# Conditioning rows formed earlier, norm sums on another engine, and two blocks' down weights in one buffer

## The chip, the cores and the metric

The kernel runs on one core of one Trainium2 chip. The metric is the device time of one execution in microseconds (us). Three timed runs of the kernel before gave 1670.92, 1672.65 and 1677.95 us, so the median is 1672.65 us. One more execution was recorded by the hardware profiler; it is the source of every row below.

A core has five instruction streams that run side by side and wait for each other through semaphores: PE (the matrix engine; its weight loads are shown as PEld), DVE (vector), ACT (scalar activation), POOL (a slower general engine) and SP (here only a queue that issues transfers). ACT and POOL issue transfers too. Each stream executes its instructions strictly in the order in which they stand: an instruction that waits holds up everything behind it on its engine, and on SP a transfer whose buffer isn't free yet holds up every later transfer of that queue.

## The reference, cut to what matters

One decoder layer on 1024 tokens of width 1024, all in float32. A conditioning vector gives six rows of 1024 numbers by one matrix product (`mod`), and these rows shift, scale and gate the two halves of the layer.

```python
cond = jax.nn.silu(c)
mod = (cond @ w_ada[layer] + b_ada[layer])[:, None, :]
sh1, sc1, gt1, sh2, sc2, gt2 = jnp.split(mod, N_MOD, axis=-1)
h = _rmsnorm(x, g_mix[layer]) * (1.0 + sc1) + sh1
x = x + gt1 * _hybrid_mixer(h, positions, rel_bias, w_in[layer], g_q_lora[layer],
                            w_uq[layer], g_kv_lora[layer], w_ukv[layer],
                            w_up_a[layer], w_up_b[layer], w_o[layer])
h = _rmsnorm(x, g_ffn[layer]) * (1.0 + sc2) + sh2
x = x + gt2 * _swiglu(h, w_gate[layer], w_up[layer], w_down[layer])
return _rmsnorm(x, g_final)
```

The mixer projects `h` by `w_in` into keys, queries, values, two gates and the latent rows `c_q` and `c_kv`; `c_q` goes through an RMS norm of its own, whose sums of squares the change touches. Two attentions follow, then `w_o`, then SwiGLU: `(silu(h @ w_gate) * (h @ w_up)) @ w_down`.

## The kernel before, in words

Activations lie transposed, features on the 128 partitions and tokens along the free axis in two halves of 512. A float32 product is made of three matmuls on a high and a low part of each operand (`split`, L82: ACT writes the high part, L83; DVE the rest, L84). The large products are done by a Strassen scheme (class `Strassen`, L168) of seven products over a 2 by 2 grid instead of eight. For that, POOL forms sums of weight quarters (`Wsum`, L190), ACT and DVE split them into operands (`Wop`, six buffers), and PE multiplies them with seven prepared operands of the right side (L220), 12 matmuls of 512 columns for a product, and 6 in the down projection. Results gather in banks of PSUM; ACT copies some out (`keep`, L163), DVE adds and combines the others (L233, L386).

The program is written in one order, and a scheduler in the compiler sets the final order of each engine's stream from it. A change at one place can therefore move instructions elsewhere too.

The stages, by the profile's time:

1. Start (0 to some 110 us): conditioning vector, first norm, the first products. The shift and scale rows of the first half are formed here (`mod_in`, L450).
2. Input projection (to 440 us): nine groups of two blocks (class `In`, loop from L702). The first eight blocks take five products each, since two were done ahead, the other ten take seven. Each block loads 1 MB of raw weights (`Wraw<-win`, L182) into one of two buffers. Beside the products run small "chores" (class `Chores`, L688): bias tables, rotary angles, the norm of `c_kv` and, by `mod_load` and `mod_run` (L666 to L678), the conditioning rows. `Chores(items, ahead, start, stop)` spreads its items over the slots from start to stop, seven slots to a group. One conditioning item handles 128 of the 1024 numbers of a row: it loads 512 KB of `w_ada` in two halves (L159, buffers `cm` and `cl` in turn), multiplies each with the conditioning vector held in two `sg` tiles (`cond_load`, L661) and sums on DVE (L675), and adds the bias (L676). In the kernel before, rows 2, 3 and 4 are formed here, 24 items from slot 30 on.
   In `cq_out` (L340) the squares of `c_q` are summed up over six blocks and two halves in `acc`; the adds stand on POOL (L348).
3. Attention (to 830 us), merge and `w_o` (to some 990 us).
4. Gate and up products (to some 1422 us): 11 pairs of blocks (class `Pair`, L1105). A pair's result is split into seven operands and stored to HBM by 14 transfers that ACT issues (`tod`, L1163). Two blocks were begun ahead and their partial results parked (`sp`), from where `post` (L1172) reloads them. In this loop (from L1206) the kernel before forms row 5, the gate of the second half: it reloads the conditioning vector (`x<-cnd`, L1205) into two of the 22 `x` buffers, and after each of the last eight pairs loads a `w_ada` block into two more and runs `mod_run`.
5. Down projection (1422 to some 1627 us): five chunks of the inner width, four blocks each (class `Down`, L1231). Two blocks run side by side, so there are ten rounds of 14 products (84 matmuls). Each block loads 512 KB of raw weights (`Wraw<-wdown`) into one of the two raw buffers of 1 MB, of which it uses half. DVE adds the result, scaled by row 5, onto the residual `x1` (L1241), which is reloaded from HBM (`x<-x1d`) as the stage begins.
6. Last blocks, final norm and output (to the end at 1674 us). Their weights (`wdl`, L1279) take a raw buffer too.

## Time and profile before

| what | value |
|---|---|
| median of three timed runs | 1672.65 us (1670.92 to 1677.95) |
| the profiled execution: its own time | 1676.03 us |
| its span, first to last instruction | 1674.2 us |
| PE busy | 1537.7 us, 92% of the span |
| PE weight loads | 1278.2 us, 76% |
| DVE busy | 1240.5 us, 74% |
| ACT busy | 829.8 us, 50% |
| POOL busy | 561.5 us, 34% |
| granted TensorE clock, mean | 0.965 of full speed |
| bytes moved | 321.92 MB, mean 192 GB/s |

A busy PE sums over the whole span; what counts in each stage is where PE stands still and what ended that. The line numbers are those of the kernel before. A row of a timeline merges equal instructions that follow each other closely. The clock has two levels, 2.4 GHz (shown as 1.00) and 1.2 GHz.

### The profile page before, as it was taken

The page shows a single profiled execution, that of the slowest core. Times are in us where ns is not written, and L with a number is a line of the kernel's source. Part 1 is how long each engine was busy: PE and PEld are TensorE (multiplying, and loading weights), DVE is VectorE, ACT ScalarE, POOL GpSimd, SP SyncE. Part 2 cuts the span into 40 slices and gives each one's busy share as a digit, 9 for nine tenths or more (in the row PEclk, how much of TensorE's full clock was granted, in tenths as well). Part 3 has the DMA queues.
Part 4 walks back from the last instruction along what each step waited for, and adds up shares of the span by engine and source line. Part 5 has one row for each costly group of instructions (what it writes and reads, how often), then busy time and mean ns, then how long its engine had stood idle before and what let it go on. Part 6 is the DMA issues. An engine that isn't in the chain of part 4 may idle for free.

```text
span 1674.2 us, 22241 instructions
## 1 busy us (share of the span) xinstructions
PE 1537.7 (92%) x7306; PEld 1278.2 (76%) x7306; DVE 1240.5 (74%) x2433; ACT 829.8 (50%) x1631; POOL 561.5 (34%) x515
## 2 busy tenths in 40 slices
PE   4989997999779989999999998989999999899996
PEld 2758786877668778999878876768888887688775
DVE  7986669576368657989866678767777786688887
ACT  5743334444467767878733563434444443222324
POOL 0143524424244546433141134322233222222323
PEclk9989999999879999999999998999999999999997
DMA  9438457558997878766195422554454449866412
GB/s 329 178 119 310 160 188 233 172 165 251 295 223 201 202 186 206 189 164 152 46 345 171 151 100 87 178 203 167 175 187 161 152 160 353 324 247 256 154 51 101
DMA packets 175652, 321.92 MB, mean 192 GB/s; under 512 B 37020, under 2 KB 72524, under 8 KB 170288
## 3 DMA queue, kind: packets, MB, share of 16 engines
q1 hardware_dynamic: 107376, 241.75, 42.2%
q0 software_dynamic: 48000, 42.04, 11.7%
q10 hardware_dynamic: 20160, 36.71, 5.8%
q8 instruction: 58, 0.95, 0.2%
q14 instruction: 58, 0.48, 0.1%
HBM read 222.73 MB, written 102.34 MB: 194 GB/s over the span
## 4 chain that ended last, share of the span: by engine, by line
PE 43%; DVE 8%; DMA 8%; ACT 3%; issue 2%; POOL 1%; ACTq 0%; SPq 0%; DVEq 0%; POOLq 0%
PE bk L220 25%; PE acc L892 3%; PE S L783 3%; PE bk L87 3%; PE bk L88 3%; PE bk L89 3%; PE pv L824 2%; DMA Wraw<-wdown 2%; DVE Wop L84 2%; PE tr L805 2%; DMA vbd<-ev 2%; DMA tod<-x 1%; DVE x L1241 1%; DVE cell L84 1%; DMA actd<-x 1%
## 5 line engine op out<-in xcount | busy, mean ns | idle before, releaser
L220 PE MATMUL bk<-cell,Wop 128*128 128x512 f32 x4056 | 951.5, 396 | 51.5 <-DVE x L233 11.0
L220 PEld LDWEIGHTS bk<-cell,Wop 128*128 128x128 f32 x4056 | 771.8, 191 | 225.1 <-ACT x L163 15.1
L190 POOL TENSOR_TENSOR Wsum<-Wraw 128x512 f32<-128x512 f32 (+1 forms) x120 | 156.4, 1304 | 599.0 <-DVE Wop L84 272.2
L83 ACT CAST Wop<-Wsum 128x512 fp32r<-128x512 f32 (+1 forms) x241 | 130.6, 550 | 198.9 <-PE bk L220 117.3
L83 ACT CAST Wop<-Wraw 128x512 fp32r<-128x512 f32 (+2 forms) x182 | 105.6, 593 | 212.4 <-PE bk L220 75.3
L84 DVE TENSOR_TENSOR Wop<-Wsum,Wop 128x512 fp32r<-128x512 f32 (+1 forms) x241 | 155.3, 653 | 61.1 <-ACT Wop L83 60.6
L84 DVE TENSOR_TENSOR Wop<-Wraw,Wop 128x512 fp32r<-128x512 f32 (+2 forms) x182 | 152.3, 843 | 39.5 <-ACT Wop L83 35.8
L783 PE MATMUL S<-cell,cell 128*128 128x128 f32 (+8 forms) x480 | 119.3, 364 | 9.7 <-DMA cell<-ksd 5.5
L1241 DVE SCALAR_TENSOR_TENSOR x<-bk,modc,x 128x512 f32<-128x512 f32 x140 | 103.5, 744 | 20.1 <-PE bk L220 18.8
L84 DVE TENSOR_TENSOR pl<-tr,ph 128x512 fp32r<-128x512 f32 (+1 forms) x160 | 98.4, 630 | 23.9 <-ACT ph L83 22.9
L790 ACT ACTIVATE P<-P,mx 128x512 f32<-128x512 f32 (+7 forms) x128 | 99.3, 778 | 29.5 <-DVE mx L785 17.6
L892 PE MATMUL acc<-cell,w 128*128 128x512 f32 x408 | 112.0, 402 | 0.1
L190 POOL TENSOR_TENSOR Wsum<-Wraw,Wsum 128x512 f32<-128x512 f32 (+1 forms) x60 | 78.5, 1313 | 68.9 <-DVE Wop L84 66.1
L805 PE MATMUL tr<-ident,P 128*128 128x128 f32 x576 | 94.1, 281 | 5.9 <-ACT P L793 5.3
L163 ACT COPY x<-bk 128x512 f32<-128x512 f32 x92 | 52.7, 588 | 91.0 <-PE bk L220 48.1
L87 PE MATMUL bk<-cell,Wop 128*128 128x512 f32 (+1 forms) x240 | 92.3, 385 | 3.7 <-ACT Wop L83 1.9
L824 PE MATMUL pv<-ph,v 128*128 128x256 f32 (+1 forms) x320 | 88.9, 294 | 6.9 <-ACT ph L83 5.6
L783 PEld LDWEIGHTS S<-cell,cell 96*128 96x128 f32 (+1 forms) x480 | 80.8, 196 | 18.6 <-DMA cell<-ksd 5.9
L88 PE MATMUL bk<-cell,Wop 128*128 128x512 f32 (+1 forms) x240 | 91.7, 383 | 0.0
L83 ACT CAST ph<-tr 128x512 fp32r<-128x512 f32 (+1 forms) x160 | 83.3, 545 | 16.3 <-PE tr L805 13.5
L89 PE MATMUL bk<-cell,Wop 128*128 128x512 f32 (+1 forms) x240 | 90.3, 379 | 0.0
L824 PE MATMUL pv<-pl,v 128*128 128x256 f32 x320 | 83.0, 294 | 4.5 <-DVE pl L84 4.1
(255 smaller groups left out, 2221.1 us busy)
## 6 DMA issues: line engine op xcount, KB each, us to landing
tod<-x ACTq DMA_DIRECT2D x140, 256.0 KB, 2.9
cell<-tod SPq DMA_DIRECT2D x70, 512.0 KB, 6.8
Wraw<-win SPq DMA_DIRECT2D x18, 1024.0 KB, 6.6
Wraw<-wgate SPq DMA_DIRECT2D x11, 1024.0 KB, 5.5
Wraw<-wup SPq DMA_DIRECT2D x11, 1024.0 KB, 6.0
Wraw<-wdown SPq DMA_DIRECT2D x20, 512.0 KB, 6.6
ada<-wada SPq DMA_DIRECT2D x16, 512.0 KB, 6.1
cell<-ksd POOLq DMA_DIRECT2D x16, 512.0 KB, 21.4
```

The lines of the kernel that those rows point to most:

```text
L83: ACT.copy(hi, src)
L84: eng.tensor_sub(lo, src, f32(hi))
L87: PE.matmul(ps, w[0], a[0], start=first, stop=False)
L88: PE.matmul(ps, w[0], a[1], start=False, stop=False)
L89: PE.matmul(ps, w[1], a[0], start=False, stop=last)
L190: POOL.tensor_tensor(t, a, b, op=op)
L220: PE.matmul(ps, w[:, wi, k], t[k][:, ti], start=start and k == 0 and n == 0, stop=k == self.nk - 1 and n == 2, skip_group_check=True)
L783: anchor[0] = PE.matmul(s, q[:, i * P:i * P + P], k[:, c * wd:c * wd + wd], start=pi == 0, stop=pi == len(passes) - 1)
L805: anchor[0] = PE.transpose(tr[:, co:co + P], self.p[a][:, kb * P:kb * P + P], ident)
L824: anchor[0] = PE.matmul(pv[:, o if l else 0:], v[:, kk], p[:, l:r], start=kk == 0 and n == 0, stop=last and l > 0 and n == 1, skip_group_c ...
L892: PE.matmul(ps, w[wi][:, k0 + k], act(k, ai, hf), start=k == 0 and n == 0, stop=k == nk - 1 and n == 2)
L1241: DVE.scalar_tensor_tensor(xs, self.bk[name], modc[:, 40 + j:41 + j], xs, op0=OP.mult, op1=OP.add)
```

## The change

Three edits.

- The ten adds of squares in `cq_out` stand on DVE instead of POOL.
- The chores form rows 2 to 5 instead of 2 to 4 (32 items instead of 24), from slot 15 on instead of 30, up to slot 58 as before. The reload of the conditioning vector and the eight `mod_run` in the gate and up loop are gone.
- In the down projection a new function `load_w` brings the weights of the two blocks of a round into the two halves of one raw buffer, and is called one round ahead: the first time before the operands of the first chunk are loaded, then as each round begins. `Down` no longer loads anything itself.

```diff
         else:
             t = X()
             ACT.activation(t, src, AF.Square)
-            POOL.tensor_add(acc[hf], acc[hf], t)
+            DVE.tensor_add(acc[hf], acc[hf], t)
...
-    mch += [(lambda j=m * 8 + k: mod_load(j, [CL(), CL()] if j % 2 else None), mod_run) for m in (2, 3, 4) for k in range(8)]
+    mch += [(lambda j=m * 8 + k: mod_load(j, [CL(), CL()] if j % 2 else None), mod_run) for m in (2, 3, 4, 5) for k in range(8)]
...
-    chores = [Chores(cch, 1, 7, 21), Chores(mch, 1, 30, 58), Chores(kch, 1, 42, 56)]
+    chores = [Chores(cch, 1, 7, 21), Chores(mch, 1, 15, 58), Chores(kch, 1, 42, 56)]
...
-    cb = X2()
-    ld2(cb, dap(cnd, 0, [[0, P], [1, D]]))
     for pr in range(2, FFB // 2):
         if pr == 2:
             p2.post()
         else:
             Pair(pr).steps(OR)
-        if pr >= 3:
-            mod_run(*mod_load(37 + pr, X2()))
...
+    def load_w(n):
+        raw = WP.tile([P, 16, P], F32, name="Wraw").rearrange("p (e q k) f -> p e q (k f)", e=2, q=4)
+        for e in range(2):
+            ld(raw[:, e], wdown[2 * n + e].rearrange("p (q r) -> p q r", q=4))
+        return raw
+
+    wnext = load_w(0)
...
-        def __init__(self, ci, dp_, ops):
+        def __init__(self, dp_, ops, raw):
             self.dp = dp_
-            super().__init__(wdown[ci * 4 + dp_], 2, ops, None, None)
+            super().__init__(None, 2, ops, None, None, False)
+            self.raw = raw
...
-            prs = [Down(ci, 2 * dd + e, ops) for e in range(2)]
+            prs = [Down(2 * dd + e, ops, wnext[:, e]) for e in range(2)]
+            if 2 * ci + dd < 2 * NC - 1:
+                wnext = load_w(2 * ci + dd + 1)
```

The built streams show three places where instructions moved. The first is PE in the third group of the input projection. `bk_` and a number is a PSUM bank in use by one quarter of a result; 1486, 1508, 1526 and 1542 belong to the third group, 1729 is the first bank of the fourth. In the kernel before:

```order
L220 MATMUL bk_1508<-cell7_972,Wop_1596 128x512 x3
L220 MATMUL bk_1729<-cell16_945,Wop_1726 128x512 x2
L220 MATMUL bk_1486<-cell8_985,Wop_1617 128x512 x3
L220 MATMUL bk_1486<-cell9_986,Wop_1617 128x512 x3
L220 MATMUL bk_1486<-cell10_987,Wop_1617 128x512 x3
L220 MATMUL bk_1486<-cell11_988,Wop_1617 128x512 x3
L220 MATMUL bk_1729<-cell16_945,Wop_1726 128x512
L220 MATMUL bk_1729<-cell17_946,Wop_1726 128x512 x2
L220 MATMUL bk_1526<-cell12_921,Wop_1657 128x512 x3
```

Two matmuls of the fourth group's first product stand ahead of the third group's last four products. At the same place of the changed kernel (the numbers are others: 1486, 1508, 1530 and 1546 are the third group's banks, 1773 is the fourth's first):

```order
L220 MATMUL bk_1508<-cell9_986,Wop_1656 128x512 x3
L220 MATMUL bk_1508<-cell10_987,Wop_1656 128x512 x3
L220 MATMUL bk_1508<-cell11_988,Wop_1656 128x512 x3
L220 MATMUL bk_1546<-cell12_921,Wop_1698 128x512 x3
L220 MATMUL bk_1546<-cell13_922,Wop_1698 128x512 x3
L220 MATMUL bk_1546<-cell14_923,Wop_1698 128x512 x3
L220 MATMUL bk_1546<-cell15_924,Wop_1698 128x512 x3
L220 MATMUL bk_1773<-cell16_945,Wop_1770 128x512 x3
L220 MATMUL bk_1773<-cell17_946,Wop_1770 128x512 x3
```

The fourth group begins when the third is through. Apart from a few such swaps in the input projection PE's order is the same to the end of the program.

The second place is the SP queue where the weights of the third group of the input projection are loaded (`rxx` are the broadcast bias tables, `cst` the rotary tables, `ksd` and `qsd` stores of keys and queries). Before:

```order
L607 DMA rxx_140<-rxd 128x1152
L336 DMA ksd_77<-x 128x512
L337 DMA ksd_77<-x 128x512
L625 DMA cst<-cl 128x128
L627 DMA cst<-cl 128x128
L182 DMA Wraw<-win 128x2048
L631 DMA cst<-cl 128x128
L159 DMA cl<-wada 128x512
L182 DMA Wraw<-win 128x2048
```

And in the changed kernel:

```order
L607 DMA rxx_140<-rxd 128x1152
L182 DMA Wraw<-win 128x2048
L611 DMA cl<-pos 128x1x128
L159 DMA cm<-wada 128x512
L159 DMA cl<-wada 128x512
L159 DMA cm<-wada 128x512
L159 DMA cl<-wada 128x512
L182 DMA Wraw<-win 128x2048
```

Four `w_ada` loads of 256 KB and the positions now stand between the two weight loads of the group. The two loads of the conditioning vector (`sg<-cnd`) stand further up, between the eight `rxx` stores.

The third place is the SP queue as the down projection begins. Before:

```order
L1220 DMA cell_13743<-tod_0_188 128x1024
L1220 DMA cell_13744<-tod_0_195 128x1024
L182 DMA Wraw<-wdown 128x1024
L1144 DMA actd_172<-x 128x512
L182 DMA Wraw<-wdown 128x1024
L1220 DMA cell_13711<-tod_6_180 128x1024
L1220 DMA cell_13712<-tod_6_187 128x1024
```

and 24 rows later, behind the whole reload of the residual, the next pair:

```order
L1220 DMA cell_14002<-tod_2_197 128x1024
L1220 DMA cell_14051<-tod_3_191 128x1024
L1220 DMA cell_14052<-tod_3_198 128x1024
L159 DMA x<-x1d_148 128x512
L182 DMA Wraw<-wdown 128x1024 x2
```

In the changed kernel both pairs stand among the operands of the first chunk, ahead of the residual's reload (`x<-x1d`):

```order
L1216 DMA cell_13711<-tod_6_187 128x1024
L1221 DMA Wraw<-wdown 128x1024 x2
L1216 DMA cell_13714<-tod_2_176 128x1024
L1216 DMA cell_13715<-tod_2_183 128x1024
L1216 DMA cell_13718<-tod_3_177 128x1024
L1216 DMA cell_13719<-tod_3_184 128x1024
L1221 DMA Wraw<-wdown 128x1024 x2
L1216 DMA cell_13741<-tod_0_188 128x1024
```

The second pair moved up by more than 20 rows, past the reload of the residual, and every later pair stands about where the pair before it stood: a round's weights are asked for one round earlier.

## Rows read from the trace of the kernel before

**Rows 1.** Busy time by stretch. Columns: the stretch and its length in us, busy time of PE, PEld, DVE, ACT and POOL in us (with the number of instructions), the granted TensorE clock, the mean busy share of the DMA engines, GB/s.

```profile
135.00:150.00 15.00, 15.00 (x68) 12.43 (x67) 9.95 (x15) 4.85 (x9) 2.92 (x2) 1.00 1.03 364
...
225.00:240.00 15.00, 15.00 (x68) 12.43 (x67) 11.52 (x23) 7.39 (x13) 7.01 (x5) 1.00 0.48 139
...
255.00:270.00 15.00, 15.00 (x68) 12.26 (x66) 15.00 (x29) 5.95 (x11) 6.46 (x4) 1.00 0.74 236
270.00:285.00 15.00, 8.10 (x34) 6.39 (x34) 15.00 (x29) 7.80 (x14) 9.01 (x6) 0.93 0.64 210
1100.00:1250.00 150.00, 149.54 (x661) 123.85 (x661) 115.85 (x160) 68.79 (x121) 46.80 (x30) 1.00 0.45 161
1250.00:1390.00 140.00, 140.00 (x619) 115.94 (x618) 110.67 (x145) 64.91 (x114) 45.69 (x30) 1.00 0.46 168
1390.00:1450.00 60.00, 49.93 (x212) 40.26 (x210) 33.67 (x57) 14.58 (x31) 9.58 (x12) 0.97 1.02 397
```

**Rows 2.** The timeline of PE in the input projection. Columns: start and length in us, engine, line, operation, output and inputs, count; in brackets the idle time in front and what ended it.

```profile
180.81 70.11 PE L220 MATMUL bk<-cell,Wop 128*128 128x512 f32 x302 [3.14 <-ACT Wop L83]
251.33 18.88 PE L220 MATMUL bk<-cell,Wop 128*128 128x512 f32 x82 [0.41 <-DVE x L386]
271.81 6.68 PE L220 MATMUL bk<-cell,Wop 128*128 128x512 f32 x28 [1.59 <-ACT x L163]
283.79 1.11 PE L359 MATMUL tr<-ident,x 128*128 128x128 f32 x4 [5.30 <-DVE x L386]
284.56 7.15 PE L220 MATMUL bk<-cell,Wop 128*128 128x512 f32 x20
293.58 11.63 PE L220 MATMUL bk<-cell,Wop 128*128 128x512 f32 x50 [1.87 <-ACT x L163]
...
371.45 10.03 PE L220 MATMUL bk<-cell,Wop 128*128 128x512 f32 x36 [3.10 <-DVE x L386]
...
393.40 46.54 PE L220 MATMUL bk<-cell,Wop 128*128 128x512 f32 x204 [1.39 <-DVE x L386]
```

**Rows 3.** The timelines of POOL and of DVE in the same stretch (columns as in rows 2).

```profile
267.10 1.69 POOL L348 TENSOR_TENSOR sg<-sg,x 128x512 f32<-128x512 f32 x1 [7.25 <-ACT x L347]
...
267.55 1.78 DVE L675 CUSTOM_DVE_ANT_0 cm<-cm,sg 128x512 f32<-128x512 f32 x1
...
283.06 0.68 DVE L386 TENSOR_TENSOR x<-bk,x 128x512 f32<-128x512 f32 x1
```

**Rows 4.** The timeline of the SP queue, that is, the issue times of its transfers, and one row of POOL's, as the weights of the third group of the input projection are loaded.

```profile
148.53 0.33 SPq L182 DMA_DIRECT2D Wraw<-win  x1
...
151.48 0.33 SPq L182 DMA_DIRECT2D Wraw<-win  x1
...
155.79 1.29 POOL L190 TENSOR_TENSOR Wsum<-Wraw 128x512 f32<-128x512 f32 x1 [17.38 <-DMA Wraw<-win]
```

**Rows 5.** Groups of instructions by line and form over the whole span: busy us, mean ns of one, then the idle time before them and what ended it.

```profile
L675 DVE CUSTOM_DVE_ANT_0 cl<-cl,sg 128x512 f32<-128x512 f32 x24 | 20.9, 873 | 7.9 <-DMA cl<-wada 7.9
...
L348 POOL TENSOR_TENSOR sg<-sg,x 128x512 f32<-128x512 f32 x10 | 16.0, 1602 | 14.1 <-ACT x L347 14.0
...
L676 DVE SCALAR_TENSOR_TENSOR modc<-mpart,badc 128x1 f32<-128x1 f32 x32 | 9.7, 305 | 0.3
...
L675 DVE CUSTOM_DVE_ANT_0 x<-x 128x512 f32<-128x512 f32 x16 | 10.8, 681 | 4.4 <-DMA tod<-x 4.0 <-DMA x<-wada 0.4
```

**Rows 6.** The timeline of PE from the second third of the gate and up products to the last blocks.

```profile
1095.65 4.36 PE L220 MATMUL bk<-cell,Wop 128*128 128x512 f32 x12 [5.27 <-DVE x L233]
1100.47 289.72 PE L220 MATMUL bk<-cell,Wop 128*128 128x512 f32 x1277 [0.46 <-DVE x L233]
...
1400.07 30.21 PE L220 MATMUL bk<-cell,Wop 128*128 128x512 f32 x132 [2.86 <-ACT x L163]
1433.61 12.51 PE L220 MATMUL bk<-cell,Wop 128*128 128x512 f32 x48 [3.32 <-DVE x L1241]
1450.30 20.87 PE L220 MATMUL bk<-cell,Wop 128*128 128x512 f32 x84 [4.18 <-ACT Wop L83]
1471.65 38.56 PE L220 MATMUL bk<-cell,Wop 128*128 128x512 f32 x168 [0.49 <-ACT Wop L83]
1510.51 38.58 PE L220 MATMUL bk<-cell,Wop 128*128 128x512 f32 x168 [0.30 <-ACT Wop L83]
1550.57 76.79 PE L220 MATMUL bk<-cell,Wop 128*128 128x512 f32 x336 [1.48 <-ACT Wop L83]
1629.15 0.47 PE L87 MATMUL bk<-cell,Wop 128*128 128x512 f32 x1 [1.79 <-DVE x L1241]
```

**Rows 7.** Single rows of the timelines of SP, ACT and DVE in the same stretch.

```profile
1086.25 0.86 SPq L159 DMA_DIRECT2D x<-cnd  x2
1087.16 3.97 SPq L1177 DMA_DIRECT2D x<-sp  x2
...
1399.44 1.08 ACT L163 COPY x<-bk 128x512 f32<-128x512 f32 x2 [10.36 <-DMA tod<-x]
...
1425.13 6.05 SPq L159 DMA_DIRECT2D x<-x1d  x6
...
1441.50 0.97 SPq L182 DMA_DIRECT2D Wraw<-wdown  x2
...
1625.33 1.23 DVE L84 TENSOR_TENSOR Wop<-Wraw,Wop 128x1024 fp32r<-128x1024 f32 x1 [1.26 <-ACT Wop L83]
```

## The prediction, made before the changed kernel ran

> **What bounds the kernel now.** I read the busy time by stretch first. From 1100 to 1390 us PE is busy 149.54 of 150 and 140.00 of 140 us [rows 1]: matmuls alone set the pace there. Then I followed the timeline of PE and looked only at rows with idle time in brackets, since PE's 12 matmuls of a product have nothing to be shortened by this change. What the edits can give back is idle PE time, and the lower clock behind some of it. At full clock a matmul takes 289.72/1277 = 0.227 us [rows 6]; every row that is slower by this measure has a stretch at the lower level in it. Two places hold nearly all of it: the input projection, and the first half of the down projection. Last I read the engines that ended each idle time, and the issue times on SP.
>
> In the input projection the worst stretch is 251 to 294 us. DVE is busy 15.00 of 15 us twice in a row, while PE falls to 8.10 of 15 [rows 1], and PE waits 0.41, 1.59, 5.30 and 1.87 us there, ended by DVE's L386 or by an ACT copy [rows 2]. So DVE is the bound for some 30 us. In front of it, at 225 to 240, DVE has 11.52 of 15 us busy and PE doesn't wait [rows 1].
>
> In the down projection PE waits 3.32, 4.18, 0.49, 0.30 and 1.48 us [rows 6], and its neighbours show why: the transfers of the second round's weights are issued only at 1441.50, behind the residual's reload that began at 1425.13 [rows 7], while the DMA engines are at 1.02 and move 397 GB/s [rows 1].
>
> **The base.** The profiled execution took 1676.03 us and its span 1674.2, the median of the three runs is 1672.65. The sums below are against the profiled one; from its time I take off 1.7 us, half of its distance to the median: 1674.3.
>
> **Down projection: -14.2 us (bounds -8 and -18).** (a) Second round. The pair of loads moves from behind the residual to the middle of the first chunk's operands. The wait of 4.18 us goes, and so does the slow start behind it: 84 matmuls in 20.87 us are 20.87 - 84 x 0.227 = 1.8 above the full clock [rows 6]. Together -6.0. Nothing else is late in its place: the first chunk's operands were in use a round earlier. (b) The later waits 0.49 + 0.30 + 1.48 [rows 6] are ended by the split of freshly loaded weights (L83); a round of notice, some 19 us, covers a load: -2.3. (c) At 1433.61 PE waits 3.32 us for L1241, which needs the residual, and 48 matmuls in 12.51 us are 1.6 above the full clock: 4.9. The reload loses 1 MB of `w_ada` in front of it (the two last conditioning blocks) and gets the second pair, also 1 MB. At 397 GB/s each is worth 2.6 us, so nothing would change but for SP, which no longer waits for `x` buffers that `w_ada` holds. I take half, -2.5; bounds 0 and -4.9. (d) At 1400.07 PE waits 2.86 us for ACT's copies, and these stood idle for 10.36 us in front, until a `tod` store was through [rows 6, 7]. In the new order of ACT these copies stand ahead of the eight stores: -2.5. (e) At 1629.15 PE waits 1.79 us; DVE's split at 1625.33 is what was late [rows 6, 7]. The last blocks' weights take a whole buffer where rounds now take one instead of two, so they can come earlier: -1.0.
>
> **Gate and up loop: -3 us (bounds 0 and -6.9).** The two loads of the conditioning vector are issued at 1086.25, directly ahead of the reload of the parked results at 1087.16 [rows 7], for which PE then waits 5.27 us, and 12 matmuls take 4.36 instead of 2.72 us [rows 6]: 6.9 in all. Without the loads the reload is issued 0.9 us earlier and shares the DMA engines with 512 KB less. The wait doesn't vanish, since the reload itself stays where it is; I take somewhat under half. The eight `mod_run` of this loop are 16 reductions, 10.8 us of DVE [rows 5], in stretches in which PE never waits [rows 1]: removing them gives nothing.
>
> **Input projection: -5.7 us (bounds -17 and +12).** Three parts gain. (f) The wait of 3.14 us at 180.81 is by order: two matmuls of the fourth group, whose weights weren't split, stood ahead of four products that were ready. In the new order they don't. With the slow part of the row behind it, 70.11 - 302 x 0.227 = 1.6 us [rows 2]: -4.7. (g) The stretch 251 to 294: the waits sum to 9.2, and 20 matmuls in 7.15 us are 2.6 above the full clock [rows 2], 11.8 in all. The rows before came at 25 items over 28 slots, 0.89 a slot; now at 33 over 43, 0.77, and a third of them is through before this stretch. I take -9, as the ten adds of L348 come in here. (h) The waits of 3.10 and 1.39 us at 371 and 393 and the slow 36 matmuls (1.9) [rows 2] fall in the last third, where 7 instead of 9 items remain: -2 of 6.4.
>
> Three parts cost. An item is two reductions of 0.68 (the undisturbed `x` form) and 0.31 us [rows 5]: 1.67 us, and 8 more are 13.4 us of DVE. An add of 128x512 on DVE takes 0.68, as L386 at 283.06 [rows 3], so ten are 6.8 us. Spread over 195 to 400 us this is 20 us in 205 us, and the row at 225 to 240 has 3.5 us in 15 free, a quarter. It fits in the mean but not everywhere: (i) +4 for places where reductions wait for their loads with the merges of PSUM banks behind them on DVE (bounds 0 and +14, twice the 6.9 us that PE loses in 270 to 285). (j) Third group's weights. In the kernel before they are issued at 148.53 and 151.48, and POOL, which must sum them, has waited 17.38 us when it starts at 155.79 [rows 4]. PE comes to this group at about 180.81 - 3.14 - six products of 2.7 = 161 us, so there is little slack. DMA is full at this time (1.03, 364 GB/s [rows 1]), and 1 MB of `w_ada`, 512 KB of vector and the positions now stand ahead of the second load: 1.5 MB at 364 GB/s are 4.3 us, and SP can also stand still until a `cm` or `cl` buffer is free. +6 (bounds 0 and +12). Sum: -4.7 - 9 - 2 + 4 + 6 = -5.7.
>
> The row behind (g) is one of the few that show the price of the adds on POOL. A reduction took 1.78 us at 267.55, while POOL's L348 ran from 267.10 for 1.69 [rows 3], against 0.68 for the `x` form, and the mean of the `cl` form is 0.87 [rows 5]. The Trainium skill (SBUF — State Buffer, "Who interferes with whom") says why that may be: DVE's second pair of SBUF ports is GpSimd's, under an exclusive lock. By that rule the move of the adds frees DVE instead of loading it, which is a rival below.
>
> **All together:** 1676.0 - 1.7 - 14.2 - 3 - 5.7 = 1651.4 us.
>
> **Rivals.** (1) *The adds free DVE.* If each L348 on POOL holds a DVE instruction back by 1.78 - 0.68 = 1.1 us, ten cost DVE 11 us now and 6.8 after: -4.2 instead of +6.8. Then the crowded stretch goes whole (-2.8 more) and (i) falls away (-4): 1644.6. For it: the row quoted. Against: it is one row, and the adds before overlapped with waits, too. 0.12. (2) *All waits go*, (i) and (j) cost nothing, and the gate and up wait goes with its slow matmuls: 1651.4 - 10 - 3.9 = 1637.5. 0.08. (3) *The down projection is bound by transfers.* The DMA engines at 1.02 can't take the second pair earlier without delaying the first chunk's operands or the residual: of (a) only the later rounds and (b) remain, about -5 of -14.2: 1660.6. Against: the 1 MB that comes in is the 1 MB that goes. 0.10. (4) *The projection eats its gain:* (j) at its bound and (i) at +8, or the crowding moved and not thinned, so the projection is at +6: 1674.3 - 17.2 + 6 = 1663.1. 0.18. (5) *Slower: DVE becomes the bound between 195 and 255 us.* The reductions there wait for their loads and hold up L386; four stretches of 15 us then look as 270 to 285 does, each 6.9 us of PE lost: 1674.3 - 17.2 + 27.6 = 1684.7. It decides once DVE's busy share passes 14 of 15 us in all four. Against it stands the quarter that is free at 225 to 240. 0.10. The Trainium skill (DMA: Bandwidth & Descriptors, "Issuing engines are not separate DMA queues") says that all issuers share the same 16 engines; the 1.03 of rows 1 agrees, and by it POOL's or ACT's issuing of a load would make (j) no smaller.
>
> **Numbers.** Forecast 0.42, rivals 0.12, 0.08, 0.10, 0.18 and 0.10. For the likeliest alone the range is 1645 to 1659. For 8 in 10 it reaches down to rival 2's edge and up past rival 4: 1638 to 1670; rival 5 and the lower part of rival 2 lie outside. Within 0.5%, 8.4 us about the median, is what a measurement of this kernel can't tell from no change: faster means under 1664.3. Forecast and rivals 1 to 3 are faster, 0.72, of rival 4 about a third more: 0.78. The rest of rival 4 and the good end of rival 5, 0.13, is the same; slower 0.09.
>
> **What would show it.** In the changed kernel's timeline of PE: no wait of over 1 us between 1440 and 1620 and the second pair of `Wraw<-wdown` issued before the first `x<-x1d` (else (a) and (b) are wrong); no wait at 180 us by the fourth group's weights (f); PE over 13 of 15 us between 255 and 285 (g); DVE under 14 of 15 us at 195 to 255 (i, against rival 5); the second `Wraw<-win` of the third group within 6 us of the first (j). L348 on DVE at 0.68 us, and the `cl` and `cm` reductions nearer 0.7 than 0.87, speak for rival 1. The forecast is wrong if the projection ends later than before, or if the first chunk's operands are what PE waits for at 1425.

## The result, and the profile after

Five timed runs of the changed kernel gave 1654.69 to 1663.36 us, median 1661.79, beside 1674.89 us (five runs, 1670.92 to 1678.67) for the kernel before. The ratio is 0.9897, 95% interval 0.9872 to 0.9921: faster by 13 to 21 us. The profiled execution was the fastest of the five, with a span of 1652.9 us against 1674.2.

Where the time went is read from PE's timeline, by four marks that both kernels have: the row of 24 matmuls at about 112 us, the first L892 (begin of attention), the row of 120 matmuls at about 1060 us (in the gate and up loop), the first matmul in the down projection that waits for a residual add, and the first L99 with four instructions after it. The stretches between them:

| stretch, us | before | changed | difference |
|---|---|---|---|
| projection: 113.40 to 439.95; 111.32 to 437.27 | 326.55 | 325.95 | -0.6 |
| attention and the rest up to 1060: 439.95 to 1061.55; 437.27 to 1057.74 | 621.60 | 620.47 | -1.1 |
| gate and up, and the first round of down: 1061.55 to 1433.61; 1057.74 to 1425.02 | 372.06 | 367.28 | -4.8 |
| down: 1433.61 to 1648.66; 1425.02 to 1629.28 | 215.05 | 204.26 | -10.8 |

The remaining 4 us lie before the first mark (2.1) and behind the last (1.9). No edit touches the start, and in the twelve runs below the first mark lies between 111.3 and 113.3 us, so this part is chance. The last part is 23.6 us in the changed kernel and 23.7 in a run below that keeps the end of the kernel before (the conditioning rows alone), so it isn't the work of the down buffer either.

The first L892 is not quite the end of the projection. It needs a load (`nqd`) that belongs to attention, and in the changed kernel PE waits 2.45 us for it. The row ahead of it, the first L783, marks the end of the projection's own products (the first two rows are from the kernel before, the others from the changed one):

```profile
439.78 0.33 PE L783 MATMUL S<-cell,cell 128*128 128x128 f32 x2
...
439.95 0.45 PE L892 MATMUL acc<-cell,wk 128*128 128x512 f32 x1
...
434.49 0.33 PE L783 MATMUL S<-cell,cell 128*128 128x128 f32 x2
...
437.27 0.47 PE L892 MATMUL acc<-cell,wk 128*128 128x512 f32 x1 [2.45 <-DMA cell<-nqd]
```

To the end of its products the projection takes 326.38 and 323.17 us, so it became 3.2 us shorter, and most of that was lost again to the wait for this load.

The timeline of PE in the second half of the changed kernel (start, length, instruction; in brackets the idle time in front and what ended it), which answers to [rows 6]:

```profile
1089.03 6.39 PE L220 MATMUL bk<-cell,Wop 128*128 128x512 f32 x26 [2.29 <-DVE x L233]
...
1425.02 184.75 PE L220 MATMUL bk<-cell,Wop 128*128 128x512 f32 x804 [5.92 <-DVE x L1245]
...
1629.28 0.61 PE L99 MATMUL tr<-ones,x 128*128 128x1 f32 x4 [1.80 <-DVE x L1319]
```

The rows of 132, 48, 84, 168, 168 and 336 matmuls of [rows 6] have become part of two unbroken ones. All waits between 1434 and 1620 us are gone, the one at 1400 too, and the one at 1090 fell from 5.27 to 2.29 us. One wait grew: that for the first residual add, from 3.32 to 5.92 us.

The same view in the projection, which answers to [rows 2]:

```profile
159.15 0.73 PE L220 MATMUL bk<-cell,Wop 128*128 128x512 f32 x2 [0.72 <-ACT Wop L83]
164.82 4.63 PE L220 MATMUL bk<-cell,Wop 128*128 128x512 f32 x10 [4.94 <-DVE Wop L84]
170.51 14.00 PE L220 MATMUL bk<-cell,Wop 128*128 128x512 f32 x60 [1.05 <-ACT Wop L83]
187.54 29.31 PE L220 MATMUL bk<-cell,Wop 128*128 128x512 f32 x122 [3.02 <-DVE x L233]
219.78 66.55 PE L220 MATMUL bk<-cell,Wop 128*128 128x512 f32 x285 [2.94 <-DVE x L233]
...
368.94 8.45 PE L220 MATMUL bk<-cell,Wop 128*128 128x512 f32 x36 [1.99 <-DVE x L386]
```

Not one wait of [rows 2] between 240 and 294 us is left. In their place stand 0.72, 4.94, 1.05, 3.02 and 2.94 us between 159 and 220. The busy time by stretch (columns as in [rows 1]) shows the same as a move:

```profile
150.00:165.00 15.00, 9.34 (x41) 7.12 (x40) 10.04 (x20) 1.24 (x2) 5.46 (x4) 0.94 0.95 345
...
195.00:210.00 15.00, 15.00 (x68) 12.43 (x67) 14.87 (x31) 5.30 (x9) 6.84 (x4) 1.00 0.69 214
210.00:225.00 15.00, 12.06 (x47) 9.50 (x46) 15.00 (x30) 2.84 (x5) 6.16 (x5) 0.89 0.76 279
225.00:240.00 15.00, 15.00 (x68) 12.39 (x67) 14.06 (x44) 4.29 (x8) 0.34 (x1) 1.00 0.86 280
240.00:255.00 15.00, 15.00 (x68) 12.43 (x67) 14.33 (x32) 8.29 (x15) 6.16 (x4) 1.00 0.68 219
255.00:270.00 15.00, 15.00 (x68) 12.43 (x67) 10.27 (x12) 8.31 (x16) 6.24 (x4) 1.00 0.57 204
270.00:285.00 15.00, 15.00 (x68) 12.42 (x67) 13.85 (x20) 9.01 (x16) 6.23 (x4) 1.00 0.47 174
```

DVE is now full from 195 to 225 us (14.87 and 15.00 of 15) and has 10.27 at 255 to 270, where it had 15.00. PE loses 2.94 us in 210 to 225 instead of 6.90 in 270 to 285, but also 5.66 in 150 to 165, where [rows 2] have no wait.

The weights of the third group, which answer to [rows 4], first on SP, then on POOL:

```profile
143.96 0.33 SPq L182 DMA_DIRECT2D Wraw<-win  x1
...
145.28 0.58 SPq L159 DMA_DIRECT2D cm<-wada  x1
...
150.88 0.33 SPq L182 DMA_DIRECT2D Wraw<-win  x1
```

```profile
155.81 1.28 POOL L190 TENSOR_TENSOR Wsum<-Wraw 128x512 f32<-128x512 f32 x1 [18.62 <-DMA Wraw<-win]
...
161.04 1.31 POOL L190 TENSOR_TENSOR Wsum<-Wraw 128x512 f32<-128x512 f32 x1 [2.59 <-DMA Wraw<-win]
```

The second load is issued 6.92 us after the first (2.95 before), four loads of `w_ada` between them. POOL begins on the first block at 155.81, as before, and on the second only at 161.04, after another wait.

### The profile page after: what moved, and what is told of

Read it like the earlier page. It is cut to its first block, busy times and chain, and to the rows that moved or that the text cites. A ratio compares the mean times of both kernels' runs of the same rounds, so it can differ in the third digit from the quotient of the medians.

```text
span 1652.9 us, 22277 instructions
## 1 busy us (share of the span) xinstructions
PE 1530.0 (93%) x7306; PEld 1273.5 (77%) x7306; DVE 1237.9 (75%) x2443; ACT 828.9 (50%) x1631; POOL 549.9 (33%) x505
## 4 chain that ended last, share of the span: by engine, by line
PE 49%; DVE 6%; DMA 6%; ACT 2%; issue 2%; POOL 1%; ACTq 0%; DVEq 0%; POOLq 0%; SPq 0%
PE bk L220 29%; PE acc L892 3%; PE S L783 3%; PE bk L87 3%; PE bk L89 3%; PE bk L88 3%; PE pv L824 2%; PE tr L805 2%; DMA vbd<-ev 2%; DMA tod<-x 1%; DMA cell<-tod 1%; DVE Wop L84 1%; DVE cell L84 1%; DMA Wraw<-wgate 1%; DVE x L278 1%
## 5 line engine op out<-in xcount | busy, mean ns | idle before, releaser
L84 DVE TENSOR_TENSOR Wop<-Wraw,Wop 128x512 fp32r<-128x512 f32 (+2 forms) x182 | 138.6, 765 | 34.5 <-ACT Wop L83 32.2
L783 PE MATMUL S<-cell,cell 128*128 128x128 f32 (+8 forms) x480 | 120.0, 365 | 13.1 <-DMA cell<-ksd 8.3
L1245 DVE SCALAR_TENSOR_TENSOR x<-bk,modc,x 128x512 f32<-128x512 f32 x140 | 103.5, 747 | 35.8 <-PE bk L220 30.9
L892 PE MATMUL acc<-cell,w 128*128 128x512 f32 x408 | 112.7, 404 | 0.1
L783 PEld LDWEIGHTS S<-cell,cell 96*128 96x128 f32 (+1 forms) x480 | 80.8, 197 | 22.1 <-DMA cell<-ksd 8.8
L892 PEld LDWEIGHTS acc<-cell,w 128*128 128x128 f32 x408 | 76.5, 193 | 13.4 <-DVE ev L923 0.4
```

What stands on the lines that cost most here:

```text
L84: eng.tensor_sub(lo, src, f32(hi))
L783: anchor[0] = PE.matmul(s, q[:, i * P:i * P + P], k[:, c * wd:c * wd + wd], start=pi == 0, stop=pi == len(passes) - 1)
L892: PE.matmul(ps, w[wi][:, k0 + k], act(k, ai, hf), start=k == 0 and n == 0, stop=k == nk - 1 and n == 2)
L1245: DVE.scalar_tensor_tensor(xs, self.bk[name], modc[:, 40 + j:41 + j], xs, op0=OP.mult, op1=OP.add)
```

## The experiments

Each kernel ran on the same chip as runs of the kernel before, and its ratio is to those. The stretches are those of the table above, from the profiled execution of each. "Projection", "gate and up" and "down" name them. The stretch of attention, which no edit touches, varied from 618 to 626 us over these runs; a single total is therefore uncertain by some 4 us. A stretch says more, but is not exact either: in kernels whose edits leave the stage alone, the projection took 323.9 to 326.1 us and gate and up 367.3 to 369.9.

**The down buffer alone.** The kernel before with this edit only:

```diff
+    wnext = load_w(0)
...
+            prs = [Down(2 * dd + e, ops, wnext[:, e]) for e in range(2)]
+            if 2 * ci + dd < 2 * NC - 1:
+                wnext = load_w(2 * ci + dd + 1)
```

> The kernel before with the shared buffer of the down weights alone. Theory A (the down weights carry nearly all of the gain, the conditioning rows only shift the projection's waits from 240-300 us to 160-220 us): 12 to 14 us below the kernel before, ratio 0.992, with no wait of PE over 1 us between the first product of the down projection and its last. Theory B (the gain comes about half from the conditioning rows): 6 to 8 us below, ratio 0.996.

Measured: ratio 0.9972 (0.9953 to 0.9991), 4.7 us, with an interval of 1.5 to 7.9: less than theory A said, and not to be told from theory B. Down took 204.16 us, all of the 10.9 that could go, but gate and up took 377.12, 5.1 more than before. Its timeline of PE shows where:

```profile
1097.43 4.99 PE L220 MATMUL bk<-cell,Wop 128*128 128x512 f32 x12 [5.62 <-DVE x L233]
...
1402.34 31.71 PE L220 MATMUL bk<-cell,Wop 128*128 128x512 f32 x132 [2.98 <-ACT x L163]
1438.53 184.65 PE L220 MATMUL bk<-cell,Wop 128*128 128x512 f32 x804 [4.47 <-DVE x L1249]
```

The wait at 1400 is there as before, and the one at the residual is 4.47 us. From the row of 132 matmuls to the one behind that wait it is 36.19 us here and 33.54 in the kernel before, so the edit takes back 2.7 us just ahead of its stage. The other 2.4 of the 5.1 lie between 1061 and 1103 us, where it doesn't reach. So theory A falls: the edit gives 10.9 us in its own stage and costs some 3 ahead of it.

**The down buffer and the adds on DVE.**

```diff
-            POOL.tensor_add(acc[hf], acc[hf], t)
+            DVE.tensor_add(acc[hf], acc[hf], t)
```

> The shared down buffer and the adds of squares on DVE, conditioning rows as in the kernel before. Theory A (adds on DVE cost about what they free): within 2 us of the run with the down buffer alone. Rival (they free DVE of the wait for POOL's port): 4 us or more below that run, and the waits of PE at 271 to 294 us shrink. Third: their 6.8 us land in a stretch where DVE is full, 5 us or more above.

Measured: 0.993 (0.991 to 0.995), 7 us below the run before, with intervals that nearly touch. In their stage, the projection, the adds changed 328.27 to 326.35 us. The waits there were 3.11, 0.87, 1.54, 5.33 and 1.36 us without them and 2.27, 0.76, 2.20 and 6.05 with them, so the bulk was not removed, as the rival would have it. 2 us or less are what the stage shows (324.41 to 323.95 to the end of its products); the other 5 us lie in stretches that this edit can't reach, and what made them is not shown. The groups of instructions by form (busy us, mean ns, idle time before; the first row is from the kernel before) show why so little:

```profile
L675 DVE CUSTOM_DVE_ANT_0 cm<-cm,sg 128x512 f32<-128x512 f32 x24 | 19.7, 835 | 3.3 <-DMA cm<-wada 3.3
...
L675 DVE CUSTOM_DVE_ANT_0 cl<-cl,sg 128x512 f32<-128x512 f32 x24 | 17.7, 737 | 6.7 <-DMA cl<-wada 6.7
...
L675 DVE CUSTOM_DVE_ANT_0 cm<-cm,sg 128x512 f32<-128x512 f32 x24 | 17.1, 724 | 4.6 <-DMA cm<-wada 4.6
...
L348 DVE TENSOR_TENSOR sg<-sg,x 128x512 f32<-128x512 f32 x10 | 8.9, 895 | 0.2 <-ACT x L347 0.2
```

The means of the reductions fell from 873 ns for `cl` [rows 5] to 737: without POOL's adds beside them they run faster (the run with the down buffer alone has 846). Over 24 instructions this is 3.3 us, and 2.7 for `cm` (835 to 724). But the ten adds now take 8.9 us of DVE themselves. The rule of the Trainium skill (SBUF — State Buffer, "Who interferes with whom") that DVE and GpSimd (POOL here) exclude each other on a pair of ports agrees with the shorter reductions; what it would give is used up by the adds.

**The changed kernel with the adds back on POOL.**

```diff
-            DVE.tensor_add(acc[hf], acc[hf], t)
+            POOL.tensor_add(acc[hf], acc[hf], t)
```

> The changed kernel with the adds of squares back on POOL. Theory A: within 2 us of the changed kernel, 1659 to 1663, ratio 0.990. Rival (the adds on DVE free it): 4 us or more above the changed kernel, 1666, with waits of PE back at 270 to 290 us. Against the run with the down buffer alone this one holds the conditioning rows alone: by theory A 3 us below it (the gate and up loop), by theory B 6 to 8 us below it.

Measured: 0.9879 (0.9858 to 0.9899), projection 325.12 us against 325.95. With the early rows the adds are worth nothing that can be measured, as theory A said. The traces show why: in the changed kernel no reduction runs between 249.4 and 320 us, and the ten adds stand from 250.9 to 317.3, so adds and reductions hardly meet any more, on whichever engine the adds are. Against the first run, this one differs by the conditioning rows: 0.9879 to 0.9972, 16 us, far more than theory A's 3. By the totals most of the gain of the whole change is theirs. By the stretches it is less, some 10 us (projection 3.2, gate and up 7.2), though the execution profiled here was the slowest of its six, 1663.44 us beside a median of 1653.82.

**The same 32 items, from slot 30 on.**

```diff
-    chores = [Chores(cch, 1, 7, 21), Chores(mch, 1, 15, 58), Chores(kch, 1, 42, 56)]
+    chores = [Chores(cch, 1, 7, 21), Chores(mch, 1, 30, 58), Chores(kch, 1, 42, 56)]
```

> The changed kernel with the 32 items from slot 30 on, as the 24 before, instead of slot 15. Theory A (a slot span too short for DVE gives waits wherever it lies; 32 items in 28 slots are 1.14 a slot): the waits of 159 to 220 us go, and those of 240 to 300 us come back larger, 15 to 20 us of PE instead of 12: 3 to 8 us above the changed kernel, 1665 to 1670. Rival (the early waits come from transfers and cost more than DVE's crowding): 3 us or more below the changed kernel.

Measured: 0.9948 (0.9928 to 0.9968), and the projection took 332.37 us, 6.4 more. PE waited 3.34 us at 281 and 7.37 at 290 and nothing over 1 us between 183 and 277. Items in fewer slots are dearer, as expected, though these two waits sum to 10.7 us and not to 15 or 20; the early start is what makes room for row 5.

**What ends the new waits: the reductions left out.**

```diff
-        for i, t in enumerate(ts):
-            DVE.tensor_tensor_reduce(t, t, cb[i], 1.0, 0.0, OP.mult, OP.add, part[:, i:i + 1])
-        DVE.scalar_tensor_tensor(modc[:, j:j + 1], part[:, 0:1], badc[:, j:j + 1], part[:, 1:2],
+        DVE.scalar_tensor_tensor(modc[:, j:j + 1], ts[0][:, 0:1], badc[:, j:j + 1], ts[1][:, 0:1],
```

> The changed kernel without the 64 reductions of the conditioning rows: all loads stay, and the small add behind them reads the loaded tiles. Rows 2 to 5 are left out of the result. In the changed kernel PE's waits between 155 and 225 us sum to 12.7 us, and its slow matmuls there to some 6 more. Theory D (DVE's time is what is short there): these waits fall to under 5 us and the stretch from the 24 matmuls at 111 us to the first of L892 from 326 to 312 to 316 us; 10 to 14 us below the changed kernel. Theory T (late weights, behind conditioning loads on SP and the DMA engines): the waits stay over 9 us, within 4 us of the changed kernel.

Measured: 0.9957 (0.9933 to 0.9981), slower in all than the changed kernel, and yet its waits between 155 and 225 us are 0.41, 2.63 and 0.99, in sum 4.0 instead of 12.7. By stretch:

```profile
180.00:195.00 15.00, 15.00 (x66) 12.15 (x65) 10.19 (x17) 6.28 (x11) 7.73 (x6) 1.00 0.95 317
195.00:210.00 15.00, 15.00 (x66) 12.17 (x65) 9.49 (x15) 4.41 (x8) 6.26 (x5) 1.00 0.96 334
210.00:225.00 15.00, 15.00 (x67) 12.14 (x66) 9.32 (x24) 4.15 (x7) 2.92 (x2) 1.00 0.77 255
```

PE doesn't wait from 180 us on, and DVE has some 5 us of 15 free. But where PE is busy for all of the 15 us, it did 66 matmuls here, and 68 in the changed kernel, at the same granted clock of 1.00. This goes through the whole execution (260 to 266 between 1200 and 1260 us), so all stretches are longer, the projection too: 319.06 us with only 4 us of waits (314.07 to the end of its products, beside 323.17). So the 10 to 14 us below the changed kernel that theory D forecast did not come. The total can't be read as a price, and what slows the matmuls was not found. The waits can: with the loads in place and the reductions gone, two thirds went, which is theory D. Of the 4.94 us at 165 about half, 2.63, stays; no run shows what holds that half, and the late weights are the likeliest.

**The loads left out, the reductions kept.**

```diff
-        ld2(ts, wada[j])
...
-            DVE.tensor_tensor_reduce(t, t, cb[i], 1.0, 0.0, OP.mult, OP.add, part[:, i:i + 1])
+            DVE.tensor_tensor_reduce(t, cb[i], cb[i], 1.0, 0.0, OP.mult, OP.add, part[:, i:i + 1])
```

> The changed kernel without the 64 loads of w_ada in the projection: the reductions stay and read the conditioning vector twice. Rows 2 to 5 are left out of the result. Theory D: the waits between 155 and 225 us stay over 8 us, since DVE has the same work; the stretch stays at 322 us or more. Theory T: they fall under 5 us, the third group's second load is issued within 2 us of the first and lands in under 8 us; 312 to 316 us. If both hold some of it, each of the two runs takes about half.

Measured: 0.9947 (0.9926 to 0.9968), with a projection of 335.41 us, 9.5 longer than with the loads. Busy time by stretch, and one row of PE's timeline:

```profile
150.00:165.00 15.00, 11.08 (x36) 8.22 (x37) 15.00 (x38) 2.80 (x5) 6.71 (x4) 0.83 0.33 123
165.00:180.00 15.00, 12.34 (x51) 9.67 (x51) 15.00 (x36) 4.59 (x8) 6.68 (x4) 0.95 0.14 53
180.00:195.00 15.00, 4.24 (x12) 3.00 (x10) 15.00 (x33) 1.41 (x3) 6.38 (x5) 0.62 0.59 210
```

```profile
198.72 100.51 PE L220 MATMUL bk<-cell,Wop 128*128 128x512 f32 x431 [14.48 <-DVE x L233]
```

With no loads to wait for, the reductions stand closer together in DVE's stream: 61 of them and their read-outs run from 150 to 195 us, beside 25 in the changed kernel. DVE was full there, and PE waited 14.48 us once for a merge on DVE. By the numbers given beforehand theory T falls. But the run doesn't price the loads, since their absence moved the reductions; it shows that DVE's queue is what PE waits for when they bunch, and that the loads had spread them out. Against theory T speaks the run before this one, where all loads are in place.

**Row 5 in the gate and up loop, but early.**

```diff
-    mch += [(lambda j=m * 8 + k: mod_load(j, [CL(), CL()] if j % 2 else None), mod_run) for m in (2, 3, 4, 5) for k in range(8)]
+    mch += [(lambda j=m * 8 + k: mod_load(j, [CL(), CL()] if j % 2 else None), mod_run) for m in (2, 3, 4) for k in range(8)]
...
             p2.post()
+            cb = X2()
+            ld2(cb, dap(cnd, 0, [[0, P], [1, D]]))
...
+        if 3 <= pr < 7:
+            for k in range(2):
+                mod_run(*mod_load(40 + 2 * (pr - 3) + k, X2()))
```

> The changed kernel, but row 5 is formed in the gate and up loop again, two items after each of the pairs 3 to 6, and its conditioning vector is loaded behind the reload of the parked results instead of ahead; rows 2 to 4 stay in the projection from slot 15 on (24 items). Theory A (what cost time in the gate and up loop was the place of two loads and the last two items, not the row): the wait at 1090 us stays near 2.3 us as in the changed kernel, none at 1400, and the projection gets 3 to 8 us shorter with 24 items; 1652 to 1658 us. Rival (row 5 costs its 5 us wherever it stands in that loop): 1661 to 1666 us.

Measured: 0.9907 (0.9892 to 0.9921), 1655.30 us, as the changed kernel. The projection with 24 items took 318.88 us, 7.1 less, as expected; gate and up took 370.56, 3.3 more, of which up to 2.6 is the spread between kernels with the same stage. The wait at 1084 was 2.20 us and none stood at 1400, so the order of two loads and the place of the last items were what cost time there, and not the row. Four new waits of 0.3 us for ACT copies, behind the pairs, took 1.2 us of it back.

**The second round's weights left out.**

```diff
-            if 2 * ci + dd < 2 * NC - 1:
+            if 0 < 2 * ci + dd < 2 * NC - 1:
```

> The changed kernel without the load of the second round's weights (the second round multiplies with the first's; its result is left out). In the changed kernel PE waits 5.92 us for the residual at 1425, 2.6 us more than before. Theory A (1 MB more of transfers stands in front of the residual, 2.6 us at 397 GB/s): the wait falls to 3 to 4 us, and 2 to 4 us in all. Rival (the residual waits for its buffers, and the second pair lies beside that): the wait stays within 1 us of 5.9.

Measured: 0.9909 (0.9885 to 0.9934), the wait at 1425 was 5.80 us. By its words the rival holds, but the run doesn't test it: its SP queue shows `Wraw<-wdown` at 1398.25 and 1402.03, ahead of the residual, since the third round's pair took the free buffer and the place of the second. The megabyte was never out of the way, so the question went to the next run.

**The second pair behind the residual.** The call that loads the pair stands behind the residual's reload in the program, and a copy of one column of the residual makes the load wait for it:

```diff
+            if behind is not None:
+                POOL.tensor_copy(raw[:, e, 0, 0:1], behind[:, 0:1])
             ld(raw[:, e], wdown[2 * n + e].rearrange("p (q r) -> p q r", q=4))
...
-            if 2 * ci + dd < 2 * NC - 1:
-                wnext = load_w(2 * ci + dd + 1)
...
+            if 2 * ci + dd < 2 * NC - 1:
+                wnext = load_w(2 * ci + dd + 1, x1[0][0] if ci == dd == 0 else None)
```

> The changed kernel, but the second round's weights are written behind a copy of one column of the residual, so that on SP their load stands behind the reload of the residual. Theory A (the megabyte in front of the residual is what made PE's wait for it grow from 3.32 to 5.92 us): that wait falls to 3 to 4 us, with at most 2 us of new waiting for the second round's weights some 20 us later; 1 to 3 us below the changed kernel. Rival (the residual waits for its buffers and for the chunk's other operands): the wait stays within 1 us of 5.9 and the second round waits in addition; not faster.

Measured: 0.9884 (0.9859 to 0.9908), not to be told from the changed kernel. Rows of PE's and of SP's timeline, and then three of SP's in the changed kernel:

```profile
1424.89 12.79 PE L220 MATMUL bk<-cell,Wop 128*128 128x512 f32 x48 [3.33 <-DVE x L1247]
1441.95 173.32 PE L220 MATMUL bk<-cell,Wop 128*128 128x512 f32 x756 [4.26 <-ACT Wop L83]
```

```profile
1417.35 6.68 SPq L159 DMA_DIRECT2D x<-x1d  x7
...
1425.00 4.98 SPq L159 DMA_DIRECT2D x<-x1d  x8
...
1433.05 2.29 SPq L1223 DMA_DIRECT2D Wraw<-wdown  x4
```

```profile
1398.14 1.55 SPq L1221 DMA_DIRECT2D Wraw<-wdown  x2
...
1415.36 0.32 SPq L159 DMA_DIRECT2D x<-x1d  x1
...
1417.86 6.66 SPq L159 DMA_DIRECT2D x<-x1d  x7
```

The wait for the residual is 3.33 us, 2.6 less than in the changed kernel, and 4.26 us stand at the second round, whose loads are now issued at 1433.05 (in the changed kernel at 1398.14); at most 2 had been expected there. Gate and up fell by 2.6 us to 364.68, and down rose by 5.6 to 209.90. By the waits, then, the megabyte in front of the residual costs 2.6 us and saves more than 4. The totals are too coarse to show the difference.

**Both, with the adds on DVE and on POOL.** The last two edits together:

> The run with row 5 formed early in the gate and up loop, and the second round's weights behind the residual. If both moves hold, 4 to 9 us below the changed kernel, ratio 0.985 to 0.987. If the residual waits for its buffers, it equals the run with row 5 early, 0.989 to 0.991.

> The run before this one with the adds of squares on POOL. The adds so far were worth 7 us (plus or minus 4) without the move of the conditioning rows and nothing with it; by the waits of PE in their stage 2 us or less both times. If they are worth 2 us or less, this run is within 3 us of the run before it. If they free DVE, it is 5 us or more slower, with waits at 270 to 290 us.

Measured: 0.9877 (0.985 to 0.9904) and 0.9881 (0.9856 to 0.9905). The projection took 318.45 and 319.76 us, so the place of the adds is worth a microsecond at most. The first ratio lies between the two that had been named, 0.987 and 0.989, and decides for neither. Whether these two beat the changed kernel stays open: their intervals overlap its own.

**The conditioning rows alone.** The kernel before with rows 2 to 5 in the projection from slot 15 on, and nothing in the gate and up loop:

```diff
-    mch += [(lambda j=m * 8 + k: mod_load(j, [CL(), CL()] if j % 2 else None), mod_run) for m in (2, 3, 4) for k in range(8)]
+    mch += [(lambda j=m * 8 + k: mod_load(j, [CL(), CL()] if j % 2 else None), mod_run) for m in (2, 3, 4, 5) for k in range(8)]
...
-    chores = [Chores(cch, 1, 7, 21), Chores(mch, 1, 30, 58), Chores(kch, 1, 42, 56)]
+    chores = [Chores(cch, 1, 7, 21), Chores(mch, 1, 15, 58), Chores(kch, 1, 42, 56)]
...
-    cb = X2()
-    ld2(cb, dap(cnd, 0, [[0, P], [1, D]]))
...
-        if pr >= 3:
-            mod_run(*mod_load(37 + pr, X2()))
```

> The kernel before with the move of the conditioning rows alone. If the edits add up, its gain is that of the run without adds less that of the run with the down buffer alone, 20 - 5 = 15 us: ratio 0.991. If the row's last loads and the second pair of down weights displace each other, so that the down buffer pays only once row 5 is out of its way, the rows alone give 6 to 9 us: ratio 0.995, with PE's 4 us wait at the second round still there.

Measured: 0.9921 (0.9894 to 0.9949), 13 us; the sum of edits (0.991) is inside the interval. The other expectation falls short of it: 0.995 is just outside, though PE's wait at the second round is there as it said. The stretches: projection 322.53 (-4.0), gate and up 365.34 (-6.7), down 215.87 (+0.8). The rows at the beginning of down:

```profile
1422.02 14.07 PE L220 MATMUL bk<-cell,Wop 128*128 128x512 f32 x48 [3.25 <-DVE x L1237]
1439.38 60.59 PE L220 MATMUL bk<-cell,Wop 128*128 128x512 f32 x252 [3.29 <-ACT Wop L83]
```

The wait of PE ahead of the first residual adds (L1241 before, L1237 here, L1245 in the changed kernel) is 3.25 us, as in the kernel before, and the second round waits 3.29. The equal lengths hide two different waits. The rows show DVE in the kernel before (two), then here, then in the changed kernel:

```profile
1431.15 0.68 DVE L675 CUSTOM_DVE_ANT_0 x<-x 128x512 f32<-128x512 f32 x1
...
1432.81 2.98 DVE L1241 SCALAR_TENSOR_TENSOR x<-bk,modc,x 128x512 f32<-128x512 f32 x4
...
1421.22 1.54 DVE L1237 SCALAR_TENSOR_TENSOR x<-bk,modc,x 128x512 f32<-128x512 f32 x2 [1.50 <-DMA x<-x1d]
...
1424.21 1.54 DVE L1245 SCALAR_TENSOR_TENSOR x<-bk,modc,x 128x512 f32<-128x512 f32 x2 [3.68 <-DMA x<-x1d]
```

In the kernel before, DVE doesn't wait for the residual at its first add. It is busy with row 5's last two reductions, which stand ahead of the add in its stream and whose weights SP issued just ahead of the residual. The residual, issued from 1425.13 on [rows 7] with 5.3 us to landing, had been there some 2 us:

```profile
1421.09 1.60 SPq L159 DMA_DIRECT2D x<-wada  x2
```

With row 5 gone, DVE and PE arrive sooner and stand waiting for the load. Counted from the end of the wait at 1090 us of each kernel, in us:

| kernel | bulk of the residual issued | PE begins to wait | DVE's wait for the residual at its first add | PE's wait |
|---|---|---|---|---|
| before | 329.5 | 334.6 | none | 3.32 |
| down buffer alone | 332.6 | 336.6 | none | 4.47 |
| rows alone | 326.9 | 330.8 | 1.50 | 3.25 |
| changed | 328.8 | 330.1 | 3.68 | 5.92 |

The rows' leaving brought the residual forward by 2.6 us, but PE by 3.8. The second pair put the residual back by 1.9 us with the rows gone and 3.2 with them there.

## Why the prediction was right or wrong

The time lies inside the range and the direction was right. The forecast of 1651.4 was too low: 22.9 us were predicted, and the interval gives 13 to 21. The median is also outside the narrower range that was given for the forecast alone, 1645 to 1659. It lies between the prices of rivals 3 and 4, but that is luck: the down stage lost 10.8 us where rival 3 left it 5, and the projection did not become longer, as rival 4 had it.

- **(a), (b), (e), the later rounds: right.** -9.3 us were worked out, and the down stretch, with its slow matmuls, became 10.8 shorter. Eight kernels hold this edit as it stands, the changed one among them; it took 204 to 205 us in seven of them, and 209 in the one with slower matmuls throughout.
- **(c), the residual: wrong in sign, and in what PE waited for.** The step read the wait of 3.32 us as one for the residual, said that the megabyte which comes is the megabyte that goes, and took -2.5. The wait grew by 2.6. In the kernel before, the residual was in place in time; the first add stood behind row 5's last reductions. Row 5's leaving did bring the residual forward, by about the 2.6 us that the step gave its megabyte, but PE came 3.8 us sooner too, so the residual became what it waits for. The megabyte that came then cost 2.6 us, which is the step's own price at 397 GB/s; the run with the pair behind the residual has 3.33 us again. This delay of the residual is the part of rival 3 that came true.
- **(d), the copies at 1400: right in size, -2.86 for -2.5.** The wait goes whenever row 5's last items leave the loop's end, and stays with the down buffer alone, so it belongs to the rows. But (c) and (d) were added up as if each stood alone: PE, which gains 2.86 us at 1400, comes that much sooner to the residual, so what the residual gained did not shorten the wait.
- **Gate and up loop: right.** The wait fell by 3.0 us, as forecast. Removing the reductions beside a full PE gave nothing that shows; only the last two had something waiting behind them, the first residual add.
- **Projection: -0.6 us by the marks and -3.2 to the end of its products, instead of -5.7.** The gains were larger than said and the costs as well. (f), (g) and (h) give the waits of [rows 2] that are gone and the slow matmuls behind them, 4.7, 11.8 and about 4, 20.5 us for 15.7 forecast. Of (f) only the ordering went: at the same border PE now waits 3.02 us for a merge on DVE. The costs were put at 10 and are 19: waits of 12.7, and 6.5 for the matmuls in these rows above 0.227 us each. Half lies before 175 us, where (j) said 6, and half at 187 and 220, where (i) said 4. Both had the right place and were undersized. The sign named for (j) was there: the second load came 6.92 us after the first, and not within 6. But transfers are at most a part of it, since without reductions 2.63 of 4.94 us stayed.
- **Rival 5 named the mechanism that took back the projection's gain,** DVE as the bound between 195 and 255 us, and its own condition was met in four of four stretches at 195 to 255 (14.87, 15.00, 14.06, 14.33). Its price was wrong: a DVE that is full cost PE 2.94 us once and not 6.9 four times. In the stretches from 195, 225 and 240 DVE is as full and PE doesn't wait at all. **Rival 1** was half right: reductions do become faster without POOL's adds, by 6.0 us in sum where it said 11, but the adds use up what that frees.
- **The sum** of the three stages, -0.6 - 4.8 - 10.8, is 16 us and inside the measured interval, while the profiled execution, the fastest, shows 21 with attention and both ends.

Two things bear on trust in this account. My first theory after the result, that the down weights carry nearly all of the gain, was read from the one profile, where the down stretch is the largest difference. It fell with the first experiment: an edit's gain in its own stage isn't its gain if it delays what stands in front. And edits do add up here within the intervals: rows alone 0.9921, down alone 0.9972, both 0.9879, where the product would be 0.9893. How the gain is shared between them is known only roughly. By totals it is 13 to 16 us for the rows and 5 to 7 for the down buffer; by the stretches some 10 for the rows and 6 to 10 for the down buffer.

## What to carry to other kernels

When a transfer is moved ahead, look at what stands right behind its new place in the queue and give that its bytes as a delay. Before a wait is put down to a load, look at the engine that ended it: here that engine was finishing small work that stood ahead, and the load had landed. And when a wait in front is taken away, ask what the engine will wait for next and whether that comes sooner too; if not, the gain moves into the next wait. Small work that is spread over a stage by the waits for its own loads can be worth more in that spread than a tighter schedule, since what PE waits for is a merge queued behind a bunch of it. And judge an edit by the stretches between fixed marks, its own and the one in front, since totals of single executions vary by several microseconds in stretches that nothing touched.

## What the runs showed of the hardware that was not expected

In the run without reductions PE did 260 matmuls of 512 columns in 60 us of unbroken work (1200 to 1260 us), against 266 in the changed kernel, both at a granted clock of 1.00. So the granted clock alone doesn't tell the rate of matmuls, and a row that is slower than 0.227 us a matmul need not hold a stretch at the lower level, as the prediction took it. The run without loads did 267 there. What makes the difference stays open.

The add on DVE took 0.68 us in nine of ten places of the changed kernel and 1.27 in one, while on POOL the same add took 1.58 to 1.60 on the mean: the groups of the changed kernel, which answer to [rows 5], show how the reductions stand beside POOL's other work now.

```profile
L675 DVE CUSTOM_DVE_ANT_0 cl<-cl,sg 128x512 f32<-128x512 f32 x32 | 25.7, 811 | 7.6 <-DMA cl<-wada 7.6
L675 DVE CUSTOM_DVE_ANT_0 cm<-cm,sg 128x512 f32<-128x512 f32 x32 | 24.8, 783 | 4.7 <-DMA sg<-cnd 3.9 <-DMA cm<-wada 0.7
...
L348 DVE TENSOR_TENSOR sg<-sg,x 128x512 f32<-128x512 f32 x10 | 7.4, 738 | 0.2 <-ACT x L347 0.2
```

The reductions kept 811 and 783 ns though POOL's adds are gone, and they have 826 and 782 with the adds back on POOL, since adds and reductions hardly meet any more. Some meet POOL's sums of weights: the one at 175.34 us took 1.78 us, while POOL summed from 174.96 on for 1.61.
